# Other start offsets within 64 bytes for the operands of a float32r projection kernel

## The chip, the cores and the metric

The kernel runs on one core of a Trainium2 chip. The metric is the device time of one execution in microseconds. Durations in the text come from one profiled execution.

## What is computed

One layer of a decoder trunk on x (512 x 1024): a normalisation with shift and scale, one wide input projection, two token mixers (a chunked mLSTM and a differential attention), their output projections, a gated merge, the output projection and a last normalisation. The input projection is by far the largest part.

```python
h = rmsnorm(x, norm_g[l]) * (1.0 + scale[:, None]) + shift[:, None]
proj = h @ w_in[l]                       # 1024 x 14344
...
ym = hm @ w_proj_m[l]                    # mLSTM branch, 2048 x 1024
ya = ha @ w_proj_a[l]                    # attention branch, 1024 x 1024
y = jax.nn.sigmoid(gm) * ym + jax.nn.sigmoid(ga) * ya
x = x + gate[:, None] * (y @ w_out[l])   # 1024 x 1024
return rmsnorm(x, final_g)
```

## The kernel before

All large products are made in float32r from operands that are split in two: hi is the value as a cast to float32r keeps it, lo is the rest. `mm3` (L133) makes a product of two split operands with three matmuls: hi with hi, lo with hi and hi with lo.

h lies transposed in SBUF as eight blocks of 128 partitions x 512 tokens, once as `h_hi` and once as `h_lo` (L339, L340). A block is 2,048 bytes of a partition. Two tiles of 32 bytes that nobody reads (`pad_before`, `pad_after`) stand around the two.

The weights come in *granules* of 128 partitions x 1024 float32 (4,096 bytes of a partition). For each, `split_granule` (L149) has SyncE load `raw`, ScalarE cast it to `whi` (L100) and VectorE subtract to get `wlo` (L118). Each of the three names has three buffers in turn. There are 112 granules of the input projection, 16 and 8 of the two branches' projections, and 8 of the output projection. The first eight of the input projection are split in the loop at L584, where h itself is made block by block; the output projection's are split in `out_weights` (L847), six of the eight not into buffers of their own but into space that is free by then: granules 0 to 2 into two blocks each of `h_hi` and `h_lo`.

A granule is used in one of two ways. In `proj_b` (L343), `attn_proj` and `proj_m` a slice of 128 columns of the granule is the stationary operand, loaded into the array by a LDWEIGHTS, and 512 columns of h (or of a branch's result, `hh` and `hl`) stream past it. A granule makes 8 x 3 matmuls of 512 columns. In `mm_v` (L354) it is the other way round: 128 tokens of a block of h are stationary and 256 columns of the granule stream. The profile writes a matmul as `acc<-h_hi,whi`: moving operand first, stationary second.

The matmuls of the two mixers (`attn_head`, `mlstm_core`, `mlstm_tail`) are generators that are advanced between granules; their place in the order of TensorE is fixed. `if_gates` (L506) takes one `whi` buffer for the weights of the input and forget gates.

Of the kernel before, what the change touches and what calls it, by code (L numbers as in the profile page):

```python
# [9 lines left out]
F32 = mybir.dt.float32  # L10
F32R = mybir.dt.float32r
# [3 lines left out]
S = 512  # L15
D = 1024
P = 128
NK = D // P
# [47 lines left out]
def hybrid_block_kernel(ctx: ExitStack, tc: tile.TileContext, xT, x, c, wada2, wada, win, wif, wpm, wpa, wout,  # L66
                        small, lamv, bif, relb, onehot, fing, out):
    nc = tc.nc
    PSUM = bass.MemoryType.PSUM
    const = ctx.enter_context(tc.tile_pool(name="const", bufs=1))  # L70
    stg = ctx.enter_context(tc.tile_pool(name="stg", bufs=3))
# [7 lines left out]
    def nm(s):  # L79
        _n[0] += 1  # L80
        return f"{s}_{_n[0]}"
# [7 lines left out]
    def core_ps():  # L89
        return core.tile([P, 512], F32, tag="core", name=nm("core"))  # L90
# [24 lines left out]
    def split(hi, lo, src, eng="act", scale=None):  # L115
        copy_r(eng, hi, src, scale)
        if scale is None:
            recent["dve"] = nc.vector.tensor_tensor(lo, src, hi.bitcast(F32), ALU.subtract)  # L118
        else:
            nc.vector.scalar_tensor_tensor(lo, src, scale, hi.bitcast(F32), ALU.mult, ALU.subtract)  # L120
# [5 lines left out]
    def inorder(inst):  # L126
        if last[0] is not None:
            tc.add_manual_dep(inst.ins, last[0].ins.name,
                              mybir.DependencyInfo(mybir.DependencyClass.NoSync, mybir.DependencyReason.DATA),
                              reason="issue order")  # L130
        last[0] = inst

    def mm3(ps, lhs, rhs, start, stop, head=False, swap=False):  # L133
        l, r = ((1, 0), (0, 1)) if swap else ((0, 1), (1, 0))
        a = nc.tensor.matmul(ps, lhs[0], rhs[0], start=start, stop=False)  # L135
        b = nc.tensor.matmul(ps, lhs[l[0]], rhs[l[1]], start=False, stop=False)  # L136
        c = nc.tensor.matmul(ps, lhs[r[0]], rhs[r[1]], start=False, stop=stop)  # L137
        last_mm[0] = c
        if head:
            inorder(a)  # L140
            inorder(b)
            inorder(c)

    def load_granule(src):
        raw = stg.tile([P, D], F32, tag="raw", name=nm("raw"))
        nc.sync.dma_start(raw, src)
        return raw

    def split_granule(src):  # L149
        raw = load_granule(src)  # L150
        hi = stg.tile([P, D], F32R, tag="whi", name=nm("whi"))
        lo = stg.tile([P, D], F32R, tag="wlo", name=nm("wlo"))
        with tc.high_priority():
            split(hi, lo, raw, eng="act")
        return hi, lo
# [16 lines left out]
    for k in range(NK):  # L172
        t = sb.tile([P, S], F32, tag="hp", bufs=16, name=nm("xt"))
# [71 lines left out]
    for i in range(2):  # L245
        ps = core_ps()
        a = nc.tensor.matmul(ps, onesf[0:1, :], crow[:, i * S:(i + 1) * S], start=True, stop=True)
# [19 lines left out]
    for k in range(NK):  # L267
        i, start = (0, k == 0) if k < 5 else (1, k == 5)
        sq = xsum[i] if start else tmp()
        a = nc.scalar.activation(sq, xt[k], AF.Square, scale=1.0 / 32)  # L270
# [17 lines left out]
    def mod_load(k):  # L288
        if k % 3 < 2:
            wa[k] = sb.tile([P, 2, D], F32, tag="p", bufs=PB, name=nm("wa"))  # L290
        else:
            wa[k] = sb.tile([P, 2, D], F32, tag="sw", name=nm("wa"))
        nc.sync.dma_start(wa[k], wada2[k])
# [13 lines left out]
    ps = core_ps()  # L307
# [21 lines left out]
    for (a, b) in ((0, 512), (512, RL)):  # L329
        ps = core_ps()  # L330
# [4 lines left out]
    nc.scalar.dma_start(rev_d, rev)  # L335


    const.tile([P, 8], F32, name="pad_before")
    h_hi = const.tile([P, NK, S], F32R, name="h_hi")  # L339
    h_lo = const.tile([P, NK, S], F32R, name="h_lo")  # L340
    const.tile([P, 8], F32, name="pad_after")

    def proj_b(col, between=None):  # L343
        hi, lo = split_granule(win[GIDX[("B", col)]])
# [239 lines left out]
    for k in range(NK):  # L584
        raw = load_granule(win[GIDX[("F", k)]]) if k > 0 else first_raw
        if k < NK - 1:
            mod_load(k + 1)
        hi = stg.tile([P, D], F32R, tag="whi", name=nm("whi"))
        lo = stg.tile([P, D], F32R, tag="wlo", name=nm("wlo"))
        a = nc.scalar.copy(hi, raw)  # L590
        issue_after(a, recent["act"])
        recent["act"] = a
        t, b = xt[k], mod[:, k:k + 1]
        x_done[0] = nc.vector.scalar_tensor_tensor(t, t, mod[:, 8 + k:9 + k], rx, ALU.mult, ALU.mult)
        in_turn(x_done[0])
        x_done[1] = recent["act"] = nc.scalar.activation(h_hi[:, k, :], t, AF.Identity, bias=b)
        in_turn(nc.vector.tensor_tensor(lo, raw, hi.bitcast(F32), ALU.subtract))
        h_dve = nc.vector.scalar_tensor_tensor(h_lo[:, k, :], t, b, h_hi[:, k, :].bitcast(F32), ALU.add,
                                               ALU.subtract)
        in_turn(h_dve)  # L600
        if k < NK - 1:
            mod_parts(k + 1)
        if k == 0:
            for a in rev_copy:
                issue_after(a, x_done[1])
        if k < NK - 2:
            issue_after(x_gain(k + 2), x_done[1])
        else:
            csl2.append(sb.tile([P, S], F32, tag="hp", bufs=16, name=nm("csl")))
            i = k - NK + 2  # L610
            nc.scalar.copy(csl2[i], csl[:, i * S:(i + 1) * S])
        for i in range(2):
            for n, f in enumerate((fq, fk)):
                ws = slice(n * 256 + i * P, n * 256 + i * P + P)
                mm3(f[i], (hi[:, ws], lo[:, ws]), (h_hi[:, k, :], h_lo[:, k, :]), k == 0, k == NK - 1,
                    swap=True)
        mm_v(fv, k, (hi[:, 512:768], lo[:, 512:768]))
        for i in range(2):
            ws = slice(768 + i * P, 768 + i * P + P)
            mm3(fz[i], (hi[:, ws], lo[:, ws]), (h_hi[:, k, :], h_lo[:, k, :]), k == 0, k == NK - 1)  # L620
        if k == 1:
            nc.sync.dma_start(lam4[:, 0:256], lamv)
            nc.sync.dma_start(bift, bif)
        if k in (5, 6):
            toe(k - 5)
        if k == 4:
            lamt = lam4[:, 256:384]
            in_turn(nc.vector.tensor_mul(lamt, lam4[:, 0:128], lam4[:, 128:256]))
            lam2 = const.tile([P, 2], F32, name="lam2")
            nc.vector.tensor_reduce(lam2, lamt.rearrange("p (a b) -> p a b", b=64), mybir.AxisListType.X, ALU.add)  # L630
            nc.scalar.activation(lam2, lam2, AF.Exp)
            nlam = const.tile([P, 1], F32, name="nlam")
            nc.vector.tensor_sub(nlam, lam2[:, 1:2], lam2[:, 0:1])
            nc.vector.tensor_scalar(nlam, nlam, -LAM_INIT, None, ALU.add)
            agc = const.tile([P, 8], F32, name="agc")
            a = nc.vector.tensor_scalar(agc, sm[:, SM_AG:SM_AG + 8], -0.5 / 256 * (1.0 - LAM_INIT), None, ALU.mult)
            mgc = const.tile([P, 16], F32, name="mgc")
            issue_after(a, h_dve)
            a = nc.vector.tensor_scalar(mgc, sm[:, SM_MG:SM_MG + 16], -0.25 / 4096, None, ALU.mult)
            issue_after(a, h_dve)  # L640
# [30 lines left out]
    for p in range(1, 4):  # L671
        for i in range(2):
# [3 lines left out]
            k = evac_ka(proj_b(C_KA + 128 * hd))  # L676
# [16 lines left out]
    ps = core_ps()  # L693
# [151 lines left out]
    wo = [None] * NK  # L845

    def out_weights(k):  # L847
        raw = stg.tile([P, D], F32, tag="raw", name=nm("raw"))
        nc.sync.dma_start(raw, wout[k])
        if k < 3:  # L850
            t = [x_[:, 2 * k:2 * k + 2, :].rearrange("p a b -> p (a b)") for x_ in (h_hi, h_lo)]
        elif k < 7:
            tag, bufs = {3: ("v", 2), 4: ("p", PB), 5: ("p", PB), 6: ("sw", 1)}[k]
            w2 = sb.tile([P, 2, D], F32R, tag=tag, bufs=bufs, name=nm("wo"))
            t = [w2[:, 0, :], w2[:, 1, :]]
        else:
            t = [stg.tile([P, D], F32R, tag=n_, name=nm(n_)) for n_ in ("whi", "wlo")]
        split(t[0], t[1], raw, eng="act")
        wo[k] = t
# [12 lines left out]
    for h in range(MH):  # L872
        q, k, v, hv = [], [], [], []
# [28 lines left out]
        for d in range(4):  # L902
            ps = proj_b(C_OM + 512 * h + 128 * d)
            while len(hv) <= d:
                tick()
            t = tmp()
# [4 lines left out]
            else:  # L911
                t = tmp()
# [14 lines left out]
    for b in range(4, 8):  # L927
        ps = proj_b(C_GM + 128 * b, tick if b > 4 else None)
# [9 lines left out]
    yt = []  # L938
# [15 lines left out]
    def rows(t):  # L954
        return slice(t * P, (t + 1) * P)

    def out_mm(ps, t, ns, ks):
        for k in ks:
            mm3(ps, (yt[k][0][:, rows(t)], yt[k][1][:, rows(t)]), (wo[k][0][:, ns], wo[k][1][:, ns]),
                k == 0, k == NK - 1)  # L960

    def residual(ps, xr, o, ns, ss):
# [10 lines left out]
    for t in range(NT):  # L973
# [5 lines left out]
        for n, ns in enumerate(parts):  # L979
            ps = first[n] if t == 0 else acc_ps() if n % 2 == 0 else core_ps()  # L980
            ps = ps[:, 0:ns.stop - ns.start]
            out_mm(ps, t, ns, range(LATE if t == 0 else 0, NK))
            o = os[ns.start // 512][:, ns.start % 512:ns.start % 512 + ns.stop - ns.start]
# [81 lines left out]
```

## Time and profile before

| | |
|---|---|
| median of the 2 runs shown | 953.75 us (953.65 to 953.86) |
| the profiled execution's own time | 953.58 us |
| its span, first to last instruction | 951.6 us |
| TensorE busy | 937.9 us, 99% |
| loading of weights (LDWEIGHTS) busy | 785.3 us, 83% |
| VectorE, ScalarE, GpSimd busy | 603.7, 457.3, 17.1 us |
| DMA, mean over the span | 121 GB/s |

The profile shows a matmul from its start to a modelled end, so two that follow each other overlap in it. The distance from start to start, which can be counted from the matmuls in a stretch, is what a matmul takes from the span. Weight loads have rows of their own (PEld) and run beside the matmul before.

### The profile page before, as it was taken

How to read it: one execution, taken by the hardware profiler on the slowest of the kernel's cores; microseconds unless marked ns; L12 is line 12 of the kernel's file. 1: busy time of each engine (PE TensorE's matmuls, PEld its weight loads, DVE VectorE, ACT ScalarE, POOL GpSimd, SP SyncE). 2: the span in 40 equal slices, each digit the busy share in tenths (PEclk: the TensorE clock that was granted, in tenths of full speed). 3: DMA queues.
4: the chain of work that ended last, by engine and by line, in shares of the span. 5: the costliest groups of instructions: out<-in, count | busy, mean ns of one | idle time of the engine just before them, and what ended most of it. 6: DMA issues, size and time to landing. Idle time of an engine off the chain costs nothing.

```text
span 951.6 us, 12250 instructions
## 1 busy us (share of the span) xinstructions
PE 937.9 (99%) x4735; PEld 785.3 (83%) x4735; DVE 603.7 (63%) x975; ACT 457.3 (48%) x741; POOL 17.1 (2%) x40
## 2 busy tenths in 40 slices
PE   7999999999999999999999999999999999999997
PEld 3887877887788789888889888898888998888886
DVE  7966777866755637534658545486554776747954
ACT  7455777756556745312436433363223653226432
POOL 0000000000001000000000000000000000000000
PEclk8999999999999999999999999999999999999999
DMA  9872313433322253343222222222231224335421
GB/s 342 318 207 88 101 67 108 147 133 123 127 72 90 85 181 111 118 147 111 89 90 89 89 89 89 89 90 91 87 111 67 89 101 147 129 127 193 166 67 67
DMA packets 40659, 114.95 MB, mean 121 GB/s; under 512 B 8289, under 2 KB 8553, under 8 KB 39578
## 3 DMA queue, kind: packets, MB, share of 16 engines
q1 hardware_dynamic: 40010, 113.11, 34.3%
q10 hardware_dynamic: 592, 1.07, 0.3%
q8 instruction: 37, 0.61, 0.3%
q14 instruction: 20, 0.16, 0.1%
HBM read 106.78 MB, written 10.00 MB: 123 GB/s over the span
## 4 chain that ended last, share of the span: by engine, by line
PE 97%; DMA 1%; ACT 1%; DVE 1%; SPq 0%; issue 0%; ACTq 0%
PE acc L135 27%; PE acc L136 26%; PE acc L137 26%; PE core L135 4%; PE core L136 4%; PE core L137 4%; PE core L442 2%; PE core L441 2%; PE core L471 1%; DMA relt<-in_relb_dram 1%; PE core L238 1%; DMA xt<-in_xT_dram 1%; DVE wlo L118 0%; ACT whi L100 0%; PE core L331 0%; PE core L492 0%
## 5 line engine op out<-in xcount | busy, mean ns | idle before, releaser
L135 PE MATMUL acc<-h_hi,whi 128*128 128x512 f32 x688 | 271.0, 394 | 0.4 <-DVE qk L410 0.4
L118 DVE TENSOR_TENSOR wlo<-raw,whi 128x1024 fp32r<-128x1024 f32 x129 | 157.8, 1223 | 171.7 <-ACT whi L100 168.0
L100 ACT CAST whi<-raw 128x1024 fp32r<-128x1024 f32 x129 | 135.5, 1050 | 271.4 <-PE acc L136 217.4
L136 PE MATMUL acc<-h_lo,whi 128*128 128x512 f32 x656 | 256.5, 391 | 0.0
L137 PE MATMUL acc<-h_hi,wlo 128*128 128x512 f32 x656 | 255.7, 390 | 0.0
L135 PEld LDWEIGHTS acc<-h_hi,whi 128*128 128x128 f32 x688 | 129.4, 188 | 29.3 <-issue 1.5
L137 PEld LDWEIGHTS acc<-h_hi,wlo 128*128 128x128 f32 x656 | 123.2, 188 | 26.2
L136 PEld LDWEIGHTS acc<-h_lo,whi 128*128 128x128 f32 x656 | 123.3, 188 | 24.0 <-issue 0.4
L135 PE MATMUL acc<-whi,h_hi 128*128 128x256 f32 x352 | 100.1, 284 | 0.0
L137 PE MATMUL acc<-whi,h_lo 128*128 128x256 f32 x352 | 99.6, 283 | 0.0
L136 PE MATMUL acc<-wlo,h_hi 128*128 128x256 f32 x352 | 99.6, 283 | 0.0
L135 PE MATMUL acc<-hh,whi 128*128 128x512 f32 x192 | 74.8, 389 | 0.0
L136 PE MATMUL acc<-hl,whi 128*128 128x512 f32 x192 | 74.8, 389 | 0.0
L137 PE MATMUL acc<-hh,wlo 128*128 128x512 f32 x192 | 74.7, 389 | 0.0
L135 PEld LDWEIGHTS acc<-whi,h_hi 128*128 128x128 f32 x352 | 67.4, 191 | 1.7 <-issue 0.8
L136 PEld LDWEIGHTS acc<-wlo,h_hi 128*128 128x128 f32 x352 | 67.4, 192 | 0.6
L137 PEld LDWEIGHTS acc<-whi,h_lo 128*128 128x128 f32 x352 | 67.4, 192 | 0.0
L444 DVE CUSTOM_DVE_ANT_0 pt<-core,bt 128x128 f32<-128x128 f32 (+3 forms) x64 | 30.3, 487 | 29.7 <-PE core L442 29.5
L446 ACT ACTIVATE pt<-pt,mn 128x128 f32<-128x128 f32 (+3 forms) x64 | 35.6, 558 | 19.7 <-DVE mn L444 19.2
L137 PEld LDWEIGHTS acc<-hh,wlo 128*128 128x128 f32 x192 | 36.0, 188 | 7.5
L135 PEld LDWEIGHTS acc<-hh,whi 128*128 128x128 f32 x192 | 36.1, 188 | 7.3
L136 PEld LDWEIGHTS acc<-hl,whi 128*128 128x128 f32 x192 | 36.1, 188 | 7.2
(276 smaller groups left out, 1363.5 us busy)
## 6 DMA issues: line engine op xcount, KB each, us to landing
raw<-in_win_dram SPq DMA_DIRECT2D x112, 512.0 KB, 3.3
wa<-in_wada_dram SPq DMA_DIRECT2D x8, 1024.0 KB, 7.4
raw<-in_wpm_dram SPq DMA_DIRECT2D x16, 512.0 KB, 3.3
raw<-in_wada_dram SPq DMA_DIRECT2D x8, 512.0 KB, 3.4
raw<-in_wpa_dram SPq DMA_DIRECT2D x8, 512.0 KB, 3.3
raw<-in_wout_dram SPq DMA_DIRECT2D x8, 512.0 KB, 3.3
gt_d<-tmp SPq DMA_DIRECT2D x12, 256.0 KB, 2.2
toe_d<-rev_d SPq DMA_DIRECT2D x8, 320.0 KB, 7.0
```

The source lines that it names most:

```text
L100: recent["act"] = nc.scalar.copy(dst, src)
L118: recent["dve"] = nc.vector.tensor_tensor(lo, src, hi.bitcast(F32), ALU.subtract)
L135: a = nc.tensor.matmul(ps, lhs[0], rhs[0], start=start, stop=False)
L136: b = nc.tensor.matmul(ps, lhs[l[0]], rhs[l[1]], start=False, stop=False)
L137: c = nc.tensor.matmul(ps, lhs[r[0]], rhs[r[1]], start=False, stop=stop)
L238: a = nc.tensor.matmul(idle, ones_r, ones_w, start=True, stop=True)
L441: inorder(nc.tensor.matmul(ps, q[m][:, qs], kh[m][:, 0:wn], start=True, stop=False))
L442: inorder(nc.tensor.matmul(ps, q[m][a, qs], kl[a, 0:wn], start=False, stop=True))
L444: nc.vector.tensor_tensor_reduce(pp, ps[:, 0:w], bt[:, S - w:S], 1.0, BIG, ALU.add, ALU.min, mn[:, qb, m:m + 1])
L446: nc.scalar.activation(pp, pp, AF.Exp, scale=-1.0, bias=mn[:, qb, m:m + 1], accum_out=ls[:, qb, m:m + 1])
L471: inorder(nc.tensor.transpose(ps[:, n:n + P], pt[:, 0, o:o + P], ident))
```

## The change

Only places in memory change, within a partition.

- h's blocks get a row of 516 instead of 512 elements, so block k begins 16 bytes x k further on within 64. The two pad tiles go.
- A granule's `whi` and `wlo` are taken from tiles that are 12 elements wider, at an offset of 0, 16, 32 or 48 bytes in turn, both at the same one (`weight_tiles`). The first eight granules and all of `split_granule` use it; the buffer of `if_gates` and granule 7 of the output projection don't.
- Output weights 0 to 2, which lie in two blocks of h, are now written and read as two parts of 512 (`wo_cols`).
- The scratch for DMA descriptors, at the start of each partition, goes to 8,192 bytes from 16,384, which makes room for the wider tiles.

```diff
+    def weight_tiles():
+        o = 4 * (turn[0] % 4)
+        turn[0] += 1
+        return [stg.tile([P, D + 12], F32R, tag=n_, name=nm(n_))[:, o:o + D] for n_ in ("whi", "wlo")]
+
     def split_granule(src):
         raw = load_granule(src)
-        hi = stg.tile([P, D], F32R, tag="whi", name=nm("whi"))
-        lo = stg.tile([P, D], F32R, tag="wlo", name=nm("wlo"))
+        hi, lo = weight_tiles()
...
-    const.tile([P, 8], F32, name="pad_before")
-    h_hi = const.tile([P, NK, S], F32R, name="h_hi")
-    h_lo = const.tile([P, NK, S], F32R, name="h_lo")
-    const.tile([P, 8], F32, name="pad_after")
+    h_hi, h_lo = (const.tile([P, NK, S + 4], F32R, name=n_)[:, :, 0:S] for n_ in ("h_hi", "h_lo"))
...
-        hi = stg.tile([P, D], F32R, tag="whi", name=nm("whi"))
-        lo = stg.tile([P, D], F32R, tag="wlo", name=nm("wlo"))
+        hi, lo = weight_tiles()
...
-            t = [x_[:, 2 * k:2 * k + 2, :].rearrange("p a b -> p (a b)") for x_ in (h_hi, h_lo)]
+            t = [x_[:, 2 * k:2 * k + 2, :] for x_ in (h_hi, h_lo)]
+            raw = raw.rearrange("p (a b) -> p a b", b=S)
...
+    def wo_cols(w, k, ns):
+        if k < 3:
+            return w[:, ns.start // S, ns.start % S:ns.start % S + ns.stop - ns.start]
+        return w[:, ns]
...
-            mm3(ps, (yt[k][0][:, rows(t)], yt[k][1][:, rows(t)]), (wo[k][0][:, ns], wo[k][1][:, ns]),
+            mm3(ps, (yt[k][0][:, rows(t)], yt[k][1][:, rows(t)]), [wo_cols(w_, k, ns) for w_ in wo[k]],
...
-    nc = _bacc.Bacc("TRN2", target_bir_lowering=False, num_devices=1)
+    nc = _bacc.Bacc("TRN2", target_bir_lowering=False, num_devices=1, dynamic_dma_scratch_size=8192)
```

Where the operands lie, from the addresses in the two built programs (bytes within a partition, modulo 64):

| | before | after |
|---|---|---|
| block k of `h_hi`, of `h_lo` | 32 | 16 x (k mod 4) |
| the buffers of `whi`, of `wlo`, of granule n | 32 | 32 + 16 x (n mod 4) |
| every other large tile that TensorE reads | 32 | 32 |
| of 4,728 pairs of a moving operand and the weights loaded for the next matmul: 0 bytes apart | 4,722 | 1,713 |
| 16 apart | 1 | 895 |
| 32 apart | 4 | 1,230 |
| 48 apart | 1 | 890 |

The order of instructions is the same on all five engines. The one difference in what stands there is the shape of six instructions on output weights 0 to 2. On ScalarE, near the end of the program, before:

```order
L100 CAST whi_7560<-raw_7558 128x1024
L930 ACTIVATE gm_7429<-acc_7392 128x512
L100 CAST h_hi<-raw_7646 128x1024
L100 CAST whi_7604<-raw_7602 128x1024
L100 CAST h_hi<-raw_7650 128x1024
```

and now:

```order
L100 CAST whi_7558<-raw_7556 128x1024
L934 ACTIVATE gm_7427<-acc_7390 128x512
L100 CAST h_hi<-raw_7644 128x2x512
L100 CAST whi_7602<-raw_7600 128x1024
L100 CAST h_hi<-raw_7648 128x2x512
```

Nothing has moved; the casts into h's blocks have two parts now, and so have the subtractions that follow them on VectorE.

## Rows read from the trace of the kernel before

**Rows 1.** The page: span, engines, granted clock by slice, the chain that ended last.

```profile
span 951.6 us, 12250 instructions
PE 937.9 (99%) x4735; PEld 785.3 (83%) x4735; DVE 603.7 (63%) x975; ACT 457.3 (48%) x741; POOL 17.1 (2%) x40
...
PEclk8999999999999999999999999999999999999999
...
PE 97%; DMA 1%; ACT 1%; DVE 1%; SPq 0%; issue 0%; ACTq 0%
```

**Rows 2.** The waits of TensorE: us in total, times, the longest.

```profile
PE core L247 <- DVE crow L244: 4.6, 1, 4.6
PE core L331 <- DMA relt<-in_relb_dram: 1.8, 1, 1.8
PE core L309 <- DVE xsum L276: 0.6, 1, 0.6
PE acc L135 <- DVE qk L410: 0.4, 1, 0.4
```

**Rows 3.** Two stretches with only 512-column matmuls: busy us (instructions) by engine, clock.

```profile
core 0: us, PE busy (x) PEld busy (x) DVE busy (x) ACT busy (x) POOL busy (x), PEclk, DMA share, GB/s
390.80:445.40 54.60, 54.60 (x242) 45.25 (x241) 20.71 (x23) 11.78 (x13) 0.00 (x0) 1.00 0.37 135
865.64:939.53 73.89, 73.89 (x327) 61.19 (x326) 53.33 (x83) 30.77 (x48) 0.00 (x0) 1.00 0.38 133
```

**Rows 4.** Timeline of TensorE in a 256-column stretch: start us, shown us, line, operation.

```profile
774.27 0.28 PE L136 MATMUL acc<-wlo,h_hi 128*128 128x256 f32 x1
774.39 0.28 PE L137 MATMUL acc<-whi,h_lo 128*128 128x256 f32 x1
...
776.19 0.28 PE L137 MATMUL acc<-whi,h_lo 128*128 128x256 f32 x1
```

**Rows 5.** ScalarE's casts and VectorE's subtractions: count, ns min/median/max, first and last start.

```profile
L100 ACT CAST whi<-raw x129: 1027/1052/1057, 60.8 to 894.9; 128x1024 fp32r<-128x1024 f32 x129
...
L100 ACT CAST hh<-z x16: 612/622/624, 508.1 to 878.1; 128x512 fp32r<-128x512 f32 x16
...
L100 ACT CAST h_hi<-raw x3: 1053/1054/1057, 881.6 to 892.3; 128x1024 fp32r<-128x1024 f32 x3
L118 DVE TENSOR_TENSOR wlo<-raw,whi x129: 1206/1225/1228, 61.9 to 904.3; 128x1024 fp32r<-128x1024 f32 x129
```

**Rows 6.** The longest wait of ScalarE: us in total, times, the longest.

```profile
ACT whi L100 <- PE acc L136: 217.4, 79, 6.3
```

**Rows 7.** Timeline of weight loads in the stretch of rows 4.

```profile
774.16 0.19 PEld L136 LDWEIGHTS acc<-wlo,h_hi 128*128 128x128 f32 x1
774.28 0.19 PEld L137 LDWEIGHTS acc<-whi,h_lo 128*128 128x128 f32 x1
```

**Rows 8.** From the chain that ended last: start us, us, ten 128-column transposes.

```profile
110.61 1.09 PE core L471 x10
```

**Rows 9.** The warm-up matmuls: their stretch with its granted clock, and their timeline.

```profile
16.77:21.75 4.98, 4.98 (x13) 3.92 (x13) 4.91 (x9) 3.02 (x5) 0.00 (x0) 0.50 1.04 415
16.77 5.35 PE L238 MATMUL core<-ones_w,ones_r 128*128 128x512 f32 x12
21.96 0.40 PE L135 MATMUL acc<-h_hi,whi 128*128 128x512 f32 x1
```

More of the change, by code (lines that the diff above doesn't have):

```diff
@@ L147, in load_granule @@
         return raw
+    turn = [0]
+    def weight_tiles():
+        o = 4 * (turn[0] % 4)
+        turn[0] += 1
+        return [stg.tile([P, D + 12], F32R, tag=n_, name=nm(n_))[:, o:o + D] for n_ in ("whi", "wlo")]
     def split_granule(src):
         raw = load_granule(src)
-        hi = stg.tile([P, D], F32R, tag="whi", name=nm("whi"))
-        lo = stg.tile([P, D], F32R, tag="wlo", name=nm("wlo"))
+        hi, lo = weight_tiles()
         with tc.high_priority():
```

## The prediction

> **What bounds the kernel now.** I read the page first. TensorE is busy 99% of the span, its granted clock is in the top digit in 39 of 40 slices, and it makes up 97% of the chain that ended last, some 923 us [rows 1]. The waits say the same from the other side: TensorE's four waits come to 7.4 us together, all but 0.4 us of it in the warm-up before the first matmul on h [rows 2]. So no other engine and no transfer sets the time; what sets it is how fast one matmul follows another.
>
> Busy time cannot show that pace, since the end of a matmul is modelled (0.28 us are shown for one that is followed by the next after 0.12 us). It has to be read from counts in long stretches of one kind. The stretch 865.64 to 939.53 us holds nothing but 512-column matmuls. 327 of them touch it, one of these begun before it, so there are 326 steps in 73.89 us: 226.7 ns each. The stretch 390.80 to 445.40 has 241 steps in 54.60 us, 226.6 ns [rows 3]. Where the granule is the moving operand (256 columns), the starts go from 774.27 to 776.19 in 16 steps: 120 ns [rows 4]. [...]
>
> [...]
>
> **The change, part by part.**
>
> *Order.* No instruction is added, removed or moved on any engine. Three casts on ScalarE and the three subtractions on VectorE that follow them, for output weights 0 to 2, get a two-part access (128x2x512 where it was 128x1024). They take 1.05 us each on ScalarE now and begin between 881.6 and 892.3 us [rows 5], while TensorE works through its unbroken stretch up to 939.5 us. If each lost as much as a second start costs (one 1,024-wide cast is 1.05 us, two 512-wide ones 2 x 0.62 us, so 0.19 us more), six of them would be 1.1 us on engines that VectorE's 72% and ScalarE's 42% busy share in that stretch leave room on [rows 3]. Cost on the path: 0, and 1.1 us without the cover.
>
> *Casts and subtractions that write at other offsets.* 129 casts of 1.05 us and 129 subtractions of 1.22 us make the granules [rows 5]. The subtractions run from 1,206 to 1,228 ns, the casts from 1,027 to 1,057, though TensorE reads at the same offset all through and the other engine now and then: a spread of 2 to 3%. I take 0. What hides a loss: one granule feeds 24 matmuls of 226.7 ns, 5.4 us, and needs 1.05 + 1.22 = 2.3 us; ScalarE stands idle 217 us in front of these casts for TensorE to give a granule's buffer back [rows 6]. The cover goes only if cast and subtraction together take over 5.4 us.
>
> *Scratch.* Halving the scratch for descriptors moves tiles down by about 7.6 to 8.2 KB and nothing else; every DMA here is issued from the queues of SyncE and ScalarE. Cost 0.
>
> *Offsets under TensorE.* This is the only term that can matter. Before, each moving operand of a matmul begins 32 bytes into its 64, and so does each stationary one but six. Of the 4,728 pairs "moving operand, and the weights that are loaded while it streams", 4,722 stand at the same offset (counted in the table under the change). After, 1,713 do; 895 are 16 bytes apart, 1,230 are 32 and 890 are 48. So **3,015 matmuls** leave the relation in which all rows of this trace were taken.
>
> What would such a matmul cost? The trace of before has no matmul of the large kinds at another relation, so I bound it. Below: it loses its whole 13.3 ns, 3,015 x 13.3 = 40.1 us. Above: it pays the 13.3 ns a second time, the nearest row that there is for a fixed cost of one matmul, plus 40.1 us. Between these ends I take **0**, for what the rows show of reads that meet. In the stretch 390.80 to 445.40 VectorE is busy 38% and ScalarE 22%; in 865.64 to 939.53 they are busy 72% and 42%, reading and writing tiles that begin at the same 32 bytes as TensorE's own; the step is 226.6 and 226.7 ns [rows 3]. Twice the traffic at the same offset costs TensorE not 0.1 ns. For TensorE's own two reads the rows don't decide: stream and load begin together, within 10 to 20 ns (a matmul at 774.27, the load of the next weights at 774.28) [rows 4, 7], so each matmul meets one load, long or short; 13.3 ns per matmul may be a cost of starting or of that one meeting. I choose the first, since a meeting of two even streams would more likely cost a varying time than 13.3 ns at each place.
>
> [...]
>
> **Sum.** 953.58 us is the profiled execution's own time (span 951.6 and 2.0 us around it), 0.17 us below the median of 953.75. 0 + 0 + 0 + 0 changes neither: **953.8 us**.
>
> **The rivals.**
>
> *Faster: the 13.3 ns come from reading in step.* [...] Against it: the two stretches of rows 3, where reads and writes of other engines at the same offset cost nothing. If the 3,015 matmuls lose all of it: 953.8 - 40.1 = 913.7 us. It is faster by over 2% (19.1 us) if each of them loses over 6.3 ns, and the rival lies between 913.7 and 934.7.
>
> [...]
>
> *Slower: reading in step is the good case.* With all operands at one offset the load and the stream can follow each other through memory without meeting twice; put 16, 32 or 48 bytes apart they may meet again and again. [...] Against it: the same rows 3. At one more fixed part for each of the 3,015: 953.8 + 40.1 = 993.9 us. It decides from 6.3 ns each (972.9 us).
>
> *The change doesn't do what it says.* A slot of the granule pool could take the 16 bytes back by its own rounding. It doesn't: slots are 4,160 bytes, 65 x 64, so all of them begin at 32 and the shift stays. The granule of the gates and the last output granule are left out of the rotation; they are 16 and 36 of the 4,735 matmuls. This gives 953.8 too.
>
> **How the numbers follow.** No effect, or one below 6.3 ns for a matmul: 0.52, since other engines' reads at the same offset are free and a cost of starting explains the 13.3 ns as well. Faster: 0.28, since the low-clock row and one payment per load fit a meeting of TensorE's two reads. Slower: 0.20; little slack at 256 columns is all that speaks for it. The likeliest case's own range is 945 to 962 (2.8 ns a matmul either way). For 8 in 10 the range takes in what it can of both others: down to 918 (four fifths of the faster case, 0.22) and up to 980 (a third of the slower, 0.07); 0.52 + 0.22 + 0.07 = 0.81. Over 2% either way is about what a measurement of this kernel can tell from no change; faster, same and slower are 0.28, 0.52 and 0.20.
>
> **What would show it.** In the trace of after, count starts in the last long stretch before the end and in a stretch of 256 columns: 226.7 and 120.0 ns say that offsets are free. If they move, h's blocks tell how, for their offset runs through all four values within a granule while the granule's stands still: steps that differ from block to block point at the relation of the two, steps alike within a granule but different between granules at the granule's own place. 1,206 to 1,228 ns for the subtractions would show that VectorE doesn't mind. The forecast is wrong if these steps change by over 6 ns on average, or if waits of TensorE for VectorE appear, which would mean that the casts got dearer.

## The result and the profile after

The changed kernel takes 963.80 us (963.07 to 964.52, two runs) where the kernel before takes 953.75: a ratio of 1.0109, 95% interval 1.0088 to 1.0129. A second measurement gave 1.0101 (1.0081 to 1.0121). So it is slower by 1.1%, by more than its interval, within the 2%, and inside the predicted range; the profiled execution has a span of 961.2 us where it was 951.6.

The page of the changed kernel, its span and its engines:

```profile
span 961.2 us, 12250 instructions
...
PE 947.8 (99%) x4735; PEld 782.9 (81%) x4735; DVE 603.9 (63%) x975; ACT 456.9 (48%) x741; POOL 16.9 (2%) x40
```

TensorE's waits (us in total, times, the longest):

```profile
PE core L254 <- DVE crow L251: 4.7, 1, 4.7
PE core L338 <- DMA relt<-in_relb_dram: 1.6, 1, 1.6
PE core L316 <- DVE xsum L283: 0.6, 2, 0.3
PE acc L135 <- DVE qk L414: 0.3, 1, 0.3
```

Against [rows 1, 2] no wait has come or gone: 7.2 us of waits where there were 7.4, VectorE and ScalarE as busy as before. TensorE alone is busy longer, by 9.9 us with the same 4,735 matmuls. The casts and subtractions kept their times (against [rows 5]; count, ns min/median/max, first and last start):

```profile
L100 ACT CAST whi<-raw x129: 1029/1048/1055, 60.4 to 902.5; 128x1024 fp32r<-128x1024 f32 x129
...
L118 DVE TENSOR_TENSOR wlo<-raw,whi x129: 1206/1225/1228, 61.4 to 912.4; 128x1024 fp32r<-128x1024 f32 x129
```

Where the time went is seen in the stretches of [rows 3], found again by counting matmuls, and in one of 256 columns (busy us and instructions by engine, granted clock, DMA):

```profile
core 0: us, PE busy (x) PEld busy (x) DVE busy (x) ACT busy (x) POOL busy (x), PEclk, DMA share, GB/s
392.76:448.47 55.71, 55.71 (x242) 45.28 (x241) 20.76 (x23) 11.79 (x13) 0.00 (x0) 1.00 0.37 132
873.68:949.23 75.55, 75.55 (x327) 61.24 (x326) 53.46 (x83) 30.40 (x48) 0.00 (x0) 1.00 0.38 131
780.76:786.25 5.49, 5.49 (x48) 5.49 (x47) 3.62 (x5) 3.04 (x5) 0.00 (x0) 1.00 0.29 96
```

241 steps in 55.71 us are 231.2 ns, 326 in 75.55 us are 231.7 ns, at the same granted clock of 1.00 and with the same work beside them: 226.6 and 226.7 before. The 256-column steps went the other way, 47 in 5.49 us, 116.8 ns, where they were 120.

Adding up all distances from one matmul's start to the next, by kind, accounts for the whole difference:

| matmuls | count | before, us | after, us | difference |
|---|---|---|---|---|
| 512 columns of h on a granule | 2,112 | 484.5 | 493.1 | +8.7 |
| 512 columns of hh and hl on a granule | 576 | 130.8 | 133.4 | +2.6 |
| output projection | 215 | 43.7 | 44.4 | +0.7 |
| 256 columns of a granule on h | 1,152 | 138.6 | 136.8 | -1.8 |
| all others | 679 | 143.0 | 142.5 | -0.5 |

Before rounding the sum is +9.6 us, and the spans differ by 9.6. Below, "step" is always such a distance, and the *relation* of a matmul is the address of its moving operand less that of the weights which are loaded beside it, those of the next matmul.

### The profile page after: what moved, and what is told of

Read it like the earlier page. It is cut to its first block, busy times and chain, and to the rows that moved or that the text cites. A ratio compares the mean times of both kernels' runs of the same rounds, so it can differ in the third digit from the quotient of the medians.

```text
span 961.2 us, 12250 instructions
## 1 busy us (share of the span) xinstructions
PE 947.8 (99%) x4735; PEld 782.9 (81%) x4735; DVE 603.9 (63%) x975; ACT 456.9 (48%) x741; POOL 16.9 (2%) x40
## 4 chain that ended last, share of the span: by engine, by line
PE 97%; DMA 1%; ACT 1%; DVE 1%; SPq 0%; issue 0%; ACTq 0%
PE acc L135 27%; PE acc L136 26%; PE acc L137 26%; PE core L135 4%; PE core L136 3%; PE core L137 3%; PE core L446 2%; PE core L445 2%; PE core L475 1%; DMA relt<-in_relb_dram 1%; DMA xt<-in_xT_dram 1%; PE core L245 0%; DVE wlo L118 0%; ACT whi L100 0%; PE core L495 0%; PE core L496 0%
## 5 line engine op out<-in xcount | busy, mean ns | idle before, releaser
L137 PE MATMUL acc<-h_hi,wlo 128*128 128x512 f32 x656 | 258.5, 394 | 0.0
L135 PE MATMUL acc<-whi,h_hi 128*128 128x256 f32 x352 | 99.5, 283 | 0.0
```

## The experiments

Three theories stood against each other at first, and a fourth, D, came up on the way. A: a step depends on the relation of the two operands. B: it depends on the granule's own place. C: the casts or subtractions, or the room made for them, cost something. D: steps are even as long as all operands share one place, and any mix upsets them.

The first ten runs below are single executions, and 17 of the kernel before lie between 952.3 and 957.2 us. So the argument rests on the steps in the traces, and the times only go along with them.

**Each half of the change alone.** First h's blocks as in the change with granules as before, then the reverse; both have the scratch of the kernel before. Both edits are shown against the changed kernel, and of the second only what concerns h's place.

```diff
-        o = 4 * (turn[0] % 4)
+        o = 0
...
-        return [stg.tile([P, D + 12], F32R, tag=n_, name=nm(n_))[:, o:o + D] for n_ in ("whi", "wlo")]
+        return [stg.tile([P, D], F32R, tag=n_, name=nm(n_))[:, o:o + D] for n_ in ("whi", "wlo")]
```

> Only h's blocks are shifted, 16 bytes more from block to block; the granules stay at 32 bytes into their 64, in slots of 4,096 bytes. In the changed kernel the 512-column steps went from 226.7 to about 232 ns and the 256-column steps from 120 to about 118. Theory A (what counts is how many bytes within 64 lie between a moving operand and the weights loaded beside it): matmuls on h are at all four relations here as in the changed kernel, so about 232 ns on h, but those on hh and hl are at relation 0 and keep 226.7 ns; about 961 us. Theory B (any weight read that is not at one fixed place in 64 breaks the even step, whatever h does): 953.8 us. Theory C (casts and subtractions at other offsets got dearer): the granules' are as before, so 953.8 us.

It takes 960.04 us (before, on the same chip: 953.78). Steps on h took 8.0 us more in all, those on hh and hl 0.1 us more. The first of the two stretches, most of which is hh, and the second:

```profile
393.19:448.11 54.92, 54.92 (x242) 45.28 (x241) 20.79 (x23) 11.85 (x13) 0.00 (x0) 1.00 0.39 134
871.41:946.24 74.83, 74.83 (x327) 61.24 (x326) 53.36 (x83) 30.84 (x48) 0.00 (x0) 1.00 0.40 132
```

54.92 us is 0.3 over the kernel before, 74.83 is 0.94 over. Moving h upsets matmuls on h and leaves those on hh alone, with granules made exactly as before: B and C can't explain it.

```diff
-    h_hi, h_lo = (const.tile([P, NK, S + 4], F32R, name=n_)[:, :, 0:S] for n_ in ("h_hi", "h_lo"))
+    const.tile([P, 8], F32, name="pad_before")
+    h_hi = const.tile([P, NK, S], F32R, name="h_hi")
+    h_lo = const.tile([P, NK, S], F32R, name="h_lo")
+    const.tile([P, 8], F32, name="pad_after")
```

> Only the granules are shifted, by 0, 16, 32 and 48 bytes in turn, in slots of 4,160 bytes; h keeps its place at 32 and the two pad tiles. Theory A (the relation within 64 bytes): a granule keeps one relation for all its 24 matmuls, so steps are even within a granule, a quarter of the granules (shift 0) at 226.7 ns and the others at whatever their relation costs; the mean is that of the changed kernel, about 232 ns on h and 231.5 on hh and hl; about 962 us. Theory B (the granule's own place): the same 962 us, with no difference between h and hh. If h's place alone counts: 953.8 us.

962.36 us. Now hh and hl are slower too, by 2.8 us in all, and h by 9.0; alone, the two halves cost 6.3 and 8.6 us, together more than the whole change. That is theory A's time, and also that of B, which the run before had ruled out. But A's detail missed: within a granule steps were not even, and no quarter of the granules kept 226.7 ns.

**No shift at all, other slots.**

```diff
-        o = 4 * (turn[0] % 4)
+        o = 0
```

(in the kernel with granules turning; tiles stay 4,144 bytes long, so slots are 4,160 bytes apart)

> The granules' slots are 4,160 bytes instead of 4,096 with no shift: every operand begins at 32 bytes within 64, as before, but granules lie at 32 or 96 within 128, and at other places within 256 and 512. Theory A (relation within 64): 953.8 us, steps of 226.7 and 120 ns. If the relation within 128 bytes or more counts: uneven steps, over 228 ns on average for 512 columns, 956 to 962 us.

964.20 us, as slow as the change itself, though every operand begins at 32 bytes within 64 as in the kernel before. The stretches:

```profile
394.38:450.09 55.71, 55.71 (x242) 45.30 (x241) 20.69 (x23) 11.71 (x13) 0.00 (x0) 1.00 0.39 132
874.98:950.33 75.35, 75.35 (x327) 61.23 (x326) 53.27 (x83) 30.72 (x48) 0.00 (x0) 1.00 0.40 131
```

So 64 bytes is not the period. Slots of 4,096 bytes had kept all granules at one place modulo 256 as well; slots of 4,160 spread them over it. In the change itself the same can be read: its steps on h are 231.6, 231.3, 231.8 and 231.6 ns on average (without those over 240 ns) where stream and weights are 0, 16, 32 and 48 bytes apart within 64.

**All of h by 16 bytes.**

```diff
-    h_hi = const.tile([P, NK, S], F32R, name="h_hi")
-    h_lo = const.tile([P, NK, S], F32R, name="h_lo")
+    h_hi, h_lo = (const.tile([P, NK * S + 16], F32R, name=n_)[:, 4:4 + NK * S].rearrange("p (k s) -> p k s", s=S)
+                  for n_ in ("h_hi", "h_lo"))
```

> All of h lies 16 bytes further on within 64 than all granules, a constant relation; the granules' slots are 4,096 bytes. Theory A (each relation within 64 has its own cost): one even step on h, other than 226.7 ns, and 226.7 on hh and hl as before; by the mean over the relations of the changed kernel up to 232 ns, about 960 us. Theory D (only a mix of relations costs, since each change of relation upsets an even rhythm): an even step of 226.7 ns on h as well, 953.8 us.

963.57 us, steps on h uneven. This run did not ask what it was meant to: its tiles are 16,448 bytes long, so h_hi and h_lo lie at 48 and 112 modulo 256, a mix and not one relation. It left A and D both standing. The next four keep every operand uniform modulo 512 except for one shift of h and one of hh and hl:

```diff
+    sb.tile([P, 8], F32, tag="pad1", name="pad1")
...
+    sb.tile([P, 120], F32, tag="pad2", name="pad2")
...
+    h_room = const.tile([P, 2 * NK * S + 144], F32R, name="h_room")
+    h_hi, h_lo = (h_room[:, o:o + NK * S].rearrange("p (k s) -> p k s", s=S)
+                  for o in (12, 12 + NK * S))
```

The first line stands ahead of hp's sixteen buffers, the second behind them, so that both together take 512 bytes. All four have the smaller scratch of the change. This is the run with h shifted by 16 bytes and hh and hl by 32; the other three have 64 and 96, 128 and 256, 256 and 192.

> No operand turns here. Before, all operands lie at one place modulo 256, in slots that are whole multiples of 512 bytes. Now h, hi and lo alike, lies 16 bytes further on than the granules, and the branches' results hh and hl lie 32 bytes further on; everything else keeps its place modulo 512. Theory D (a uniform relation keeps an even step, and only operands that differ among themselves modulo 256 upset it): even steps of 226.7 ns for 512 and 120 for 256 columns on h and on hh, 953.8 us. Theory A, widened (each relation has its own step): even steps, but others than 226.7: on h one value for 16, on hh one for 32; by the changed kernel up to 232 ns, 953.8 + 2,700 x 5.2 ns = 968 us at most.

That of 16 and 32 takes 964.85 us.

> As the run with 16 and 32 bytes, but h lies 64 and hh and hl 96 bytes further on than the granules modulo 256. Theory D: 953.8 us, steps of 226.7 and 120 ns. Theory A, widened: other even steps; if it is the place within 64 that counts, h keeps 226.7 and hh doesn't; if within 128 or 256, neither does.

That of 64 and 96 takes 958.09 us.

> As before, with h 128 and hh and hl 256 bytes further on than the granules (modulo 512, h was 256 bytes away and hh 0 in the kernel before). Theory D: 953.8 us. Theory A, widened: hh keeps 226.7 ns, as h had it at 256; h keeps 226.7 if the period is 128 bytes and not if it is 256.

That of 128 and 256 takes 964.94 us.

> As before, with h moved by 256 bytes, so that it lies at the granules' own place modulo 512, and hh and hl 192 bytes further on than the granules. Theory D: 953.8 us. Theory A, widened: h keeps 226.7 ns (hh had it at this relation before), hh changes unless the period is 64 bytes.

That of 256 and 192 takes 956.91 us (before: 953.24 for the four). D falls: with nothing mixed, one uniform shift changes the step. The first stretch, mostly hh, of the run of 128 and 256:

```profile
395.44:450.38 54.94, 54.94 (x242) 45.24 (x241) 20.78 (x23) 11.83 (x13) 0.00 (x0) 1.00 0.38 134
```

The same stretch and the one of 256 columns, of the run of 256 and 192:

```profile
390.00:445.89 55.89, 55.89 (x242) 45.10 (x241) 20.71 (x23) 11.75 (x13) 0.00 (x0) 1.00 0.36 132
775.82:781.44 5.62, 5.62 (x48) 5.62 (x47) 3.74 (x5) 3.17 (x5) 0.00 (x0) 1.00 0.28 93
```

The stretch of 256 columns, of the run of 64 and 96:

```profile
775.75:781.10 5.35, 5.35 (x48) 5.35 (x47) 3.47 (x5) 2.90 (x5) 0.00 (x0) 1.00 0.30 98
```

hh at 256 keeps 226.7 ns and at 192 takes 233.3, step after step. In the timeline of the run of 256 and 192:

```profile
395.13 0.39 PE L135 MATMUL acc<-hh,whi 128*128 128x512 f32 x1
...
397.47 0.39 PE L136 MATMUL acc<-hl,whi 128*128 128x512 f32 x1
```

There are ten steps between these two rows, 2.34 us. With h at 256 all of h's steps are those of the kernel before (5.62 us for the 47 of 256 columns above, where 47 x 120 ns are 5.64). So a shift of 256 is no shift, 128 is one (h: 232.8 ns), and the relation modulo 256 is what counts. At other relations the steps don't vary at random but repeat a short rhythm: 230, 228, 234, 235 for 16 bytes, 226, 229, 232 for 64.

**A table of all relations.**

```diff
+        o = 4 * (5 * turn[0] % 16)
+        turn[0] += 1
+        return [stg.tile([P, D + 64], F32R, tag=n_, name=nm(n_))[:, o:o + D] for n_ in ("whi", "wlo")]
```

(in the kernel before, with the smaller scratch; `split_granule` and the loop of the first eight granules call it, as in the change)

> A table of the relation between stream and weights. h and the branches' results keep their place; each granule, hi and lo alike, begins 80 bytes further on than the one before it, modulo 256, so that all sixteen multiples of 16 bytes come in turn; a granule keeps its place for its 24 or 48 matmuls, and slots are 4,352 bytes, 17 x 256. Theory A, widened (the step is set by the place of the moving operand less that of the weights, modulo 256): 512-column steps by that difference as the uniform runs have them, 226.7 ns at 0, 231.7 at 16, 233.3 at 32, 229 at 64, 233.3 at 96, 232.5 at 128, 233.3 at 192, on h and on hh alike; 256-column steps 120 at 0, 113.3 at 192, about 118 at 240; the mean over all sixteen is near the 232 and 118 ns of the changed kernel, so about 962 us. Theory D (what costs is that operands differ from each other): since a granule's matmuls do not differ among each other but for their start, 226.7 and 120 ns inside a granule, about 954 us.

963.27 us (before: 952.19). Mean steps in ns, of matmuls with at least six of the same relation ahead of them; in the table column with 512 columns those on h, in the uniform column those of the four runs above, h or hh. The values of the table at 0 and 64 with 256 columns rest on six and five matmuls, all others of it on forty or more:

| relation mod 256 | 512 columns, table | 512, uniform | 256 columns, table | 256, uniform |
|---|---|---|---|---|
| 0 | 227.0 | 227.0 | 120.0 | 120.0 |
| 16 | 227.7 | 231.8 | 118.7 | |
| 32 | 233.3 | 233.3 | | |
| 48 | 232.0 | | 118.3 | |
| 64 | 229.6 | 230.4 | 117.8 | |
| 80 | 230.1 | | 119.5 | |
| 96 | 233.2 | 233.4 | | |
| 112 | 229.5 | | 113.9 | |
| 128 | 232.4 | 232.8 | | 119.4 |
| 144 | 233.3 | | 118.6 | |
| 160 | 234.2 | | 117.4 | |
| 176 | 232.0 | | 119.3 | |
| 192 | 233.3 | 233.3 | 113.4 | 113.7 |
| 208 | 233.4 | | 119.2 | |
| 224 | 233.4 | | 118.4 | |
| 240 | 232.0 | | 117.1 | 118.4 |

Here the weights moved and in the uniform runs the stream did, and yet six of the seven 512-column pairs of numbers agree to within 0.8 ns: it is the difference that counts and not either place. (The weights of one granule all lie at one place, so these runs don't tell the next matmul's weights from its own.) For 512 columns relation 0, which is the kernel before, is the best of the sixteen; for 256 columns it is the worst, and 192 the best. The sixteen 512-column values have a mean of 231.7 ns, and 231.6 is what the changed kernel's steps on h come to. That fits the account of the change: it spreads the matmuls over the relations.

The pair that disagrees (16 bytes: 227.7 and 231.8) shows that the relation does not settle all. There is more than one rhythm for it, and some means of the table lie between two paces. In the table granules at 16 bytes ran at 226.7 or 228.4 ns, those at 112 at 226.6 or 233.2, and one of five at 240 at 226.6 where the others took 233.3; with all of h at 64 bytes, granules ran at 229 or 233.4. Only at relation 0 did every granule settle at 226.7. Place alone does not choose the rhythm: the 20th and the 68th granule lie in the same buffers at the same offset, 16 bytes from h, and ran at 226.6 and 228.4. What is left is what came before, and a repetition below shows a case of it.

**Control, a better version, and the change again.** The control is the kernel of the table with o = 0: smaller scratch, wider slots, no shift. The version shifts only the granules that stream, by 48 elements or 192 bytes (`split_granule` takes the offset):

```diff
-        hi, lo = split_granule(win[GIDX[("A", col, half)]])
+        hi, lo = split_granule(win[GIDX[("A", col, half)]], 48)
```

> A control for everything in the change but the offsets: the scratch for descriptors is 8,192 bytes and the granules' slots are 4,352 bytes (17 x 256), but every granule begins at the start of its slot, so that all operands lie at one place modulo 256 as before. Theory A: steps of 226.7 and 120.0 ns, 953 to 954 us. If the smaller scratch or other slots cost by themselves: over 956 us.

954.00 us (before: 954.01); steps of 226.7 and 119.8 ns in the two long stretches and in the one of 256 columns:

```profile
391.40:446.03 54.63, 54.63 (x242) 45.25 (x241) 20.72 (x23) 11.77 (x13) 0.00 (x0) 1.00 0.38 135
866.25:940.14 73.89, 73.89 (x327) 61.19 (x326) 53.33 (x83) 30.80 (x48) 0.00 (x0) 1.00 0.39 133
774.76:780.39 5.63, 5.63 (x48) 5.62 (x47) 3.74 (x5) 3.18 (x5) 0.00 (x0) 1.00 0.28 93
```

The smaller scratch and wider slots that keep their places modulo 256 cost nothing.

> A version that should beat both: as the control, but granules that stream (256 columns, from the second stage on) begin 192 bytes into their slot, and those whose slices are the weights stay at 0. By the table of the scan the 256-column steps fall from 120.0 to 113.3 or 113.4 ns and the 512-column ones stay at 226.7. Theory A: 1,056 matmuls x 6.6 ns = 7.0 us less, about 946.5 us, ratio 0.9926. Theory D (any difference costs): 953.8 us or more.

950.75 us, ratio 0.9968 (0.9953 to 0.9982): faster than both kernels, but by 3.3 us and not by 7. The 512-column steps stayed, as A has it. Of 22 stretches of 256-column matmuls, 4 ran at 113.3 ns and 18 at 117.8. One of each, 36 steps:

```profile
106.34:110.41 4.07, 4.07 (x38) 4.07 (x37) 3.52 (x8) 2.71 (x8) 0.32 (x1) 1.00 0.65 190
772.93:777.16 4.23, 4.23 (x38) 4.23 (x37) 3.42 (x4) 1.78 (x5) 0.00 (x0) 1.00 0.37 124
```

At the same relation of 192 the run with h at 64 bytes had 21 of 22 at 113.3. There the matmuls ahead of a stretch were upset, and a stretch began with some steps of 113 to 125 ns before it settled. Here most of them are even and at relation 0, and the stretch falls straight into the slower rhythm. That this is the reason was not tested, and how to choose the rhythm was not tried.

> The changed kernel a second time. If addresses alone set each step (theory A), the steps repeat one by one to within a nanosecond or two, wherever casts and loads fall: 512 columns on h about 232 ns on average, 256 about 118, 963 to 965 us. If the uneven steps come from meetings with the other engines or with transfers, the order of the single steps differs from that of the first profile while the mean stays.

964.51 us, ratio 1.0101 (1.0081 to 1.0121). 99.5% of its 4,734 steps are within 2 ns of the same step in the first profile; the two stretches take the same 55.71 and 75.55 us:

```profile
392.19:447.90 55.71, 55.71 (x242) 45.32 (x241) 20.77 (x23) 11.77 (x13) 0.00 (x0) 1.00 0.38 132
873.11:948.66 75.55, 75.55 (x327) 61.30 (x326) 53.48 (x83) 30.52 (x48) 0.00 (x0) 1.00 0.39 131
```

Uneven as the steps look, they are set by the program and not by meetings with other engines or transfers. The 26 steps that differ by more lie in the warm-up and in one granule behind a wait at 69.4 us: the step with the wait took 721 ns in the first profile and 713 in the second, and the 21 steps after it ran in another order, at 234.0 and 235.6 ns on average. So in this one case the same program at the same addresses took another rhythm behind a wait that differed by 8 ns.

## Why the prediction was right, and where it was not

*What bounds the kernel* held: the waits are 7.2 us where they were 7.4 and the whole difference, 9.6 us, is in the steps. *Order*, *casts and subtractions* and *scratch* held at 0: the subtractions are at 1,206 to 1,228 ns to the nanosecond, and the control with less scratch is 954.0.

*Offsets under TensorE* is the term that was mis-sized: taken as 0, it is +9.6 us, all of it. So the class came out right with the wrong mechanism, which is luck: 963.8 us lies outside the likeliest case's own 945 to 962 and inside only the range that was widened for the rivals. The kernel stayed within 2% only because the effect is small, 4.1 ns for a matmul on h and 4.5 on hh, where the text had set 6.3 ns as the point from which it would decide. Three readings in that part were wrong.

- I took the 13.3 ns for a cost of starting, because a meeting of two streams would cost a varying time. A cost that hangs on two addresses can be just as even: at relation 0 the runs give an even 226.7 ns, at 32 and 192 averages of 233.3, the same for granule after granule. The two are 6.6 ns apart, and 113.3 and 120.0 are 6.7. No run shows the 13.3 ns, of which the 40.1 us on either side of the forecast are made, as a fixed part of a matmul. At relation 0 the two steps leave it over if every column costs the same, 2 x 120.0 - 226.7 = 13.3; but at 192 the same sum is 2 x 113.4 - 233.3 = -6.5, which no fixed cost can be. What the changed kernel showed in its place is 4.1 ns more for a matmul on h, 4.5 more on hh and 1.6 less at 256 columns.
- That other engines' traffic is free at the same offset, which [rows 3] show (226.6 ns with VectorE busy 38%, 226.7 with 72%), says nothing on TensorE's own two reads. The table doesn't bear out a term of 0: by relation the mean step of 512 columns goes from 227.0 to 234.2 ns. What is lost there, no run shows.
- I counted relations within 64 bytes, as the change is laid out. The run with no shift and slots of 4,160 bytes shows that this count of 3,015 meant nothing; the period is 256. (The last output granule, by the way, is in 27 matmuls and not in 36; nothing hangs on that.)

Of the rivals the slower one had the right dependence for 512 columns: reading in step, 227.0 ns, is the good case, and granules and h apart cost more (its reason, a second meeting in memory, is not shown). Its price was too high, 4 to 5 ns on average and not 13.3; the little slack at 256 columns that was to speak for it is not shown either, and just these matmuls got faster. The faster rival had a piece of truth there: at 256 columns reading in step is the bad case (120.0 ns, and 113.4 at relation 192), and the change gave back 1.8 us. The low-clock row that its chance was set by has 432 ns for a matmul at a granted clock of 0.50 [rows 9], 21 ns under twice 226.7; what makes the difference, no run shows. The sign to look for, steps that differ from block to block, did appear, as rhythms; but it does not tell the two cases apart as I had thought, for in the table steps differ within a granule whose relation stands still.

What stays open is why 256 bytes are the period and what makes a rhythm of a few matmuls. That the weights' load and the stream meet in memory was my own reading of a step that depends on their difference; no run here shows such a meeting.

## What to carry to other kernels

Where TensorE is busy throughout, read its pace as starts counted in stretches of one shape, and compare it between places of the operands: at a granted clock of 1.00 it hung on addresses here. In float32r keep the streaming operand and the weights loaded beside it at the same place modulo 256 bytes for 512 columns (227.0 ns here, and up to 234.2 at other places), and beware of tile sizes that aren't a multiple of that, since padding a tile by 48 bytes (slots 64 bytes wider) cost as much here as shifting it (964.20 and 963.80 us). An offset chosen for one shape is not the one for another (here 0 for 512 columns and 192 bytes for 256); scan it with one kernel that turns through all of them, before arguing about one, and then measure the chosen one in place: the 113.4 ns of the table became 117.8 in most stretches of the version.

## What had not been expected of the hardware

- A 512-column float32r matmul took 227.0 to 234.2 ns on average, and a 256-column one 113.4 to 120.0 ns, by the difference modulo 256 bytes between the stream and the next weights, at a granted clock of 1.00.
- Slots of 4,160 instead of 4,096 bytes, nothing else, took the kernel from 953.78 to 964.20 us.
- At one relation there can be two or three stable rhythms: 113.3 and 117.8 ns at 192 bytes with 256 columns, 226.7, 228.4 and 231.8 at 16 bytes with 512. The same ones run again from one execution to the next, but for the one granule behind a wait that differed by 8 ns.
